# Encoder block on one core: softmax sums carried through the meta keys' transposes, division on GpSimd in each attention unit

## The chip, the core and the metric

The kernel runs on one core of one Trainium2 chip. The metric is the device time of one execution in microseconds (us). TensorE (PE in the profile; PEld is its weight load) multiplies matrices into PSUM, VectorE (DVE) and ScalarE (ACT) read PSUM and SBUF, GpSimd (POOL) here works on SBUF alone, and the SyncE queue (SP) issues most DMAs. Each engine executes its own instructions in order and waits for others through semaphores.

## What is computed

One encoder layer over two batches, a prompt of 256 and a sample of 1024 tokens, each with 16 learned meta tokens in front (lengths 272 and 1040), width 1024, all fp32. Cut to what matters:

```python
h = rms_norm(x, g);  z = h @ w_in            # q | k | v | fourier | two gates
q, k = rope(head_rms_norm(q)), rope(head_rms_norm(k))   # 8 query heads, 2 key/value heads, 64 wide
s = einsum('bqhgd,bshd->bhgqs', qb, k) * scale
p = softmax(s, axis=-1)                      # over all 272 or 1040 keys
a = einsum('bhgqs,bshd->bqhgd', p, v).reshape(..., 512) @ w_attn_o
fo = fourier_mix(f) @ w_four_o
x = x + (sigmoid(g_attn) * a + sigmoid(g_four) * fo) @ w_out
x = x + swiglu_ffn(rms_norm(x));  y = rms_norm(x)       # meta tokens dropped from the output
```

The softmax's division by the sum of the exponentials commutes with the product with v, so it may be applied to the attention output a instead.

## The kernel before

Precision: each fp32 operand of a large product is split into a rounded high part and a low remainder, and three matmuls (L231 to L233) make one product. Work is emitted by Python generators. In the attention the order on PE, ACT and DVE is the order written in the code; DMAs on SP and work on POOL are placed by the framework's scheduler.

**Stages.** First come the norms, transposes, Fourier part and the passes for q and k/v (to about 324 us in the profile); then the attention (324 to about 681), then the merge of the two branches (`merge`, `load_af`), `w_out`, and the feed-forward network to the end.

**Attention** (`attention`, L861 to L1010). A unit is one tile t of 128 queries with one key/value head g: four query heads h. The tiles come in the order 8, 9 (prompt), 0 to 7 (sample), so there are 20 units, 4 of the prompt. For each head: six matmuls (two for the prompt) write the scores into `S` (L960; for the sample one buffer of three PSUM banks, L955); DVE takes the row maximum (L965); ACT takes the exponential into the SBUF slot `p` and, by `accum_out`, the row sum into one column of the small tile `total` (L973). The next head's scores must wait until that exponential has read `S`.

The other half of a unit, `Second`, runs while the next unit's scores run. A `turn` (L889) transposes one block of 128 keys (the ninth block, or third for the prompt, holds the 16 meta keys) of the four heads into a PSUM tile `pt`; ACT rounds it to `pT` (L895), DVE subtracts for the low part (L896). `product` (L906) comes two turns later and adds the block to `pv`, a single PSUM bank of 128 x 512: its upper 64 rows are the product with the high part of v, its lower the other. After the last block ACT copies one half to the slot `ao` (L920), DVE adds the other half (L921), and a DMA stores the sum in DRAM, in `a_d` (L924). In each head `turns(0)` comes behind the maximum and `turns(1)` behind the exponential. Between them the generator yields, and a filler emits matmuls of the gates (`g`, L231 to L233), whose weights are split on ACT and POOL (L578, L579).

**The divisors before.** While the next unit runs, `divide` is called: in its head 1 DVE takes the reciprocals of `total` (L991); in head 2 PE transposes them into a free corner of `S` (L994), DVE copies that (L996), and two DMAs store it in `rc_d` (L999). For the last unit both calls stand ahead of the drain (L1001, L1002). The exponential of head 2 is emitted behind that call.

**Reading a^T back.** `load_af` (L1058) loads 1024 columns of `a_d` (L1070) and the divisors, which a DMA spreads over 64 partitions twice (L1073); DVE multiplies (L1080), and `split` makes the high and low parts (L215, L216). It runs five times: two for chunk 0 (tiles 0 to 3), one for chunk 2 (the prompt), two for chunk 1 (tiles 4 to 7). The merge uses them in the order 0, 2, 1: matmuls `m` behind matmuls `fo` of the Fourier branch.

**Slots.** SBUF is handed out by `Slots` (27 slots of 1056 columns and 7 triples), the one freed longest ago first; whoever writes a slot waits for its last user.

The queries are loaded by `load_q` (L868) from `q_d`, one tile ahead; the first load is emitted when the attention begins.

Of the kernel before, what the change touches and what calls it, by code (L numbers as in the profile page):

```python
# [9 lines left out]
F32 = mybir.dt.float32  # L10
F32R = mybir.dt.float32r
AF = mybir.ActivationFunctionType
ALU = mybir.AluOpType
# [4 lines left out]
P = 128  # L18
# [4 lines left out]
HD = 64  # L23
# [11 lines left out]
CH_N = (512, 512, 256)  # L35
# [22 lines left out]
SLOT = 1056  # L58
# [78 lines left out]
def f32(ap):  # L137
    return ap.bitcast(F32)
# [44 lines left out]
class Kernel:  # L183
    def __init__(self, tc, nc, a, o, pools):
        self.tc, self.nc, self.a, self.o = tc, nc, a, o
        self.const, self.small, self.dram, big = pools
        self.later = None
        self.sl = Slots(big, N_SLOTS, N_TRIPLES)
        c = self.const
        self.ident = c.tile([P, P], F32, name="ident")  # L190
        nc.scalar.dma_start(self.ident[:], a["ident"])
        self.gcol = c.tile([P, KD], F32, name="gcol")
        self.mhalf = c.tile([P, NQH], F32, name="mhalf")
        nc.vector.memset(self.mhalf[:], -0.5)
        self.gates = [
            [self.dram.tile([P, n], F32, name=f"gate{u}_{i}") for i, n in enumerate(CH_N)]
            for u in range(16)
        ]
        self.x_d = [self.dram.tile([P, D], F32, name=f"x_d{t}") for t in range(10)]
        self.act_d = [[self.dram.tile([P, 640], F32, name=f"act_d{j}_{k}") for k in range(NH)] for j in range(7)]  # L200
        self.q_d = [self.dram.tile([P, D], F32, name=f"q_d{t}") for t in range(10)]
        self.a_d = [self.dram.tile([512, n], F32, name=f"a_d{i}") for i, n in enumerate(CH_N)]

        self.rc_d = [self.dram.tile([2, 4 * n], F32, name=f"rc_d{i}") for i, n in enumerate(CH_N)]


        self.f_d = self.dram.tile([516, NL], F32, name="f_d")
# [553 lines left out]
    def kv_pass(self, ps):  # L761
# [14 lines left out]
        for c, off, rows, t in self.TILES[10:] + self.TILES[8:10] + self.TILES[:8]:  # L776
# [33 lines left out]
            if late:  # L810
                late()
                yield 500
            late = post
        yield 8000
        late()
        sl.put(self.rope)
# [41 lines left out]

    def attention(self, ps, tiles, tag_s, tag_v):  # L861


        nc, sl = self.nc, self.sl
        units = [(t, g) for t in tiles for g in range(NKV)]
        q = {}

        def load_q(i):  # L868
            if i < len(tiles) and tiles[i] not in q:
                s = sl.get("qT", F32R)  # L870
                nc.sync.dma_start(f32(s[:, :1024]), self.q_d[tiles[i]][:])
                q[tiles[i]] = s

        load_q(0)

        class Second:

# [11 lines left out]
            def turn(me):  # L889
                V, rows, col = me.keys[me.j]  # L890
                pt = ps.tile([P, 512], F32, tag="tr", name=f"pt{me.t}{me.g}{me.j}")
                for h in range(4):
                    nc.tensor.transpose(pt[:rows, h * P : (h + 1) * P], me.ps4[h][:, col : col + rows], self.ident[:])  # L893
                pT = sl.get("pT", F32R)
                nc.scalar.copy(pT[:rows, :512], pt[:rows, :])  # L895
                nc.vector.tensor_tensor(pT[:rows, 512:1024], pt[:rows, :], f32(pT[:rows, :512]), op=ALU.subtract)  # L896
                if len(late) == 2:
                    product()
                late.append((me, me.j, pT))
                me.j += 1  # L900
                if me.j == len(me.keys):
                    sl.put(*me.slots)
# [3 lines left out]
        def product():  # L906
# [10 lines left out]
                return  # L917
            aos = sl.get("ao")

            nc.scalar.copy(aos[:HD, :512], me.pv[HD:P, :])  # L920
            nc.vector.tensor_tensor(aos[:HD, :512], me.pv[:HD, :], aos[:HD, :512], op=ALU.add)  # L921
            off = (t % 4) * P if t < 8 else (t - 8) * P
            dst = self.a_d[t // 4][:].rearrange("(h d) n -> d h n", d=HD)
            nc.sync.dma_start(  # L924
# [16 lines left out]

        for i, (t, g) in enumerate(units):
            if g == 0:
                load_q(tiles.index(t) + 1)
            if t < 8:
                seq, L, cuts = "s", LS, (0, 264, 776, LS)
            else:
                seq, L, cuts = "p", LP, (0, LP)
            per = SLOT // L
            ps4, slots = [], []  # L950
            total = self.small.tile([P, 4], F32, tag="total", name=f"total{t}{g}", bufs=3)
            for h in range(4):
                hq = q[t][:, (4 * g + h) * P : (4 * g + h + 1) * P]

# [9 lines left out]
                nb = sm[:, 0:1]  # L964
                nc.vector.tensor_reduce(nb, S[:, base : base + L], axis=AX.X, op=ALU.max, negate=True)  # L965
                turns(0)
                if divide and h:
                    divide(S[:4, 0:P] if t < 8 else S[:4, base + 384 : base + 512])
                    divide = None if h == 2 else divide
                if h % per == 0:  # L970
                    slots.append(sl.get("p"))
                p = slots[-1][:, (h % per) * L : (h % per + 1) * L]
                self.last_exp = nc.scalar.activation(p, S[:, base : base + L], AF.Exp, bias=nb, accum_out=total[:, h : h + 1])  # L973
                yield "end" if i + 1 == len(units) else seq, 0, False

                ps4.append(p)
                turns(1)
# [6 lines left out]
                if t == tiles[-1]:  # L984
                    sl.put(*self.kv_slots[:4])
            queue.append((Second(t, g, ps4, slots), n + 1))

            def divide(bank, t=t, g=g, total=total, first=[]):

                if not first:  # L990
                    first.append(nc.vector.reciprocal(total[:], total[:]))  # L991
                    return
                c, off = t // 4, t % 4 * P
                nc.tensor.transpose(bank, total[:], self.ident[:])  # L994
                rc = self.small.tile([4, P], F32, tag="rcT", name=f"rcT{t}{g}")
                nc.vector.tensor_copy(rc[:], bank)  # L996
                for x in range(2):
                    dst = self.rc_d[c][x].rearrange("(k n) -> k n", k=4)[2 * g : 2 * g + 2, off : off + P]
                    nc.sync.dma_start(dst, rc[x::2, :])  # L999

        divide(None)  # L1001
        divide(ps.tile([P, 512], F32, tag="tr", name="rcT")[:4, :P])  # L1002
        while queue:
            for half in range(2):
                turns(half)
# [52 lines left out]
    def load_af(self, c):  # L1058

        nc, sl = self.nc, self.sl  # L1060
        n = CH_N[c]
        per = 1024 // n
        out = self.af[c] = []
        raws = {}

        def load(i):
            if i < 4 // per:
                r, d = raws[i] = sl.get("af"), sl.get("rc")
                src = self.a_d[c][i * per * P : (i + 1) * per * P, :].rearrange("(k p) n -> p k n", p=P)
                nc.sync.dma_start(r.v(per, n), src)  # L1070
                for x in range(2):
                    src = self.rc_d[c][x, i * 1024 : (i + 1) * 1024]
                    nc.sync.dma_start(d[x * HD : (x + 1) * HD, :1024], src.partition_broadcast(HD))  # L1073

        load(0)
        yield 1
        for i in range(4 // per):
            load(i + 1)
            r, d = raws.pop(i)
            nc.vector.tensor_tensor(r[:, :1024], r[:, :1024], d[:, :1024], op=ALU.mult)  # L1080
            out.append(self.split(r, 1024, "af", nc.vector, "t"))
            sl.put(r, d)
            yield 1

    def merge(self, then):
# [854 lines left out]
```

## Time and profile before

| | us |
|---|---|
| median of 3 runs (1744.39 to 1746.44) | 1744.83 |
| the profiled execution's own time | 1742.25 |
| its span, first to last instruction | 1740.5 |
| PE busy | 1667.6 |
| DVE busy | 1093.8 |
| ACT busy | 724.4 |
| POOL busy | 302.8 |

A time in the timeline is counted from the span's start. A row of the timeline is start, duration, engine, line, operation, output and inputs, and in brackets the idle time of the engine just before it with what ended it. A row of the waits is engine, tile and line, what it waited for, the total, the number of times, and the longest. A row of the windows gives the busy time of each engine in a stretch, the clock granted to TensorE (1.00 is full), the busy share of the 16 DMA engines and their GB/s. A matmul's row shows its whole passage; back to back, one with 512 columns starts 0.23 us after the one before it.

### The profile page before, as it was taken

Reading aid. Unit: us, or ns where it says so; the run is one execution under the profiler, and the core shown is the slowest. Engines: PE = TensorE matmul, PEld = TensorE weight load, DVE = VectorE, ACT = ScalarE, POOL = GpSimd, SP = SyncE. Lnnn points to the kernel's source line nnn. Section 1 sums busy time; section 2 is a strip of 40 time slices with the busy share of each in tenths; the row PEclk is TensorE's granted clock in tenths of the full one; section 3 lists DMA queues with packets and bytes.
Section 4 is the critical chain, followed back from the end, with each engine's and each line's share of the span. In section 5 each row is a group of like instructions: output and inputs, shape, how many; then the busy total and the mean of one; then the engine's idle time right before and its main releaser. Section 6 shows DMA issues by size and latency. Waiting matters only on the chain.

```text
span 1740.5 us, 25983 instructions
## 1 busy us (share of the span) xinstructions
PE 1667.6 (96%) x9809; PEld 1479.5 (85%) x9809; DVE 1093.8 (63%) x1973; ACT 724.4 (42%) x1462; POOL 302.8 (17%) x348
## 2 busy tenths in 40 slices
PE   7999999989999999899999999999999999999998
PEld 7888879767777777787879999999999998888886
DVE  5563455346666666663379766676666668775685
ACT  6423233346565665442254322232222234443444
POOL 3350443210021111564244000000000000000002
PEclk9999999999999999899999999999999999999999
DMA  6145221321111218634441223222222237653534
GB/s 244 43 121 176 97 110 58 110 67 51 44 45 41 75 40 244 179 110 169 145 173 61 85 85 102 90 90 93 96 90 87 75 126 253 199 177 105 157 98 154
DMA packets 91581, 198.62 MB, mean 114 GB/s; under 512 B 10006, under 2 KB 41474, under 8 KB 91456
## 3 DMA queue, kind: packets, MB, share of 16 engines
q1 hardware_dynamic: 81552, 179.54, 31.3%
q10 hardware_dynamic: 8400, 12.53, 2.1%
q0 software_dynamic: 1504, 4.89, 0.9%
q8 instruction: 77, 1.26, 0.3%
q14 instruction: 48, 0.39, 0.1%
HBM read 141.46 MB, written 55.46 MB: 113 GB/s over the span
## 4 chain that ended last, share of the span: by engine, by line
PE 60%; DVE 9%; ACT 4%; issue 4%; POOL 2%; DMA 2%; SPq 0%; POOLq 0%; ACTq 0%; DVEq 0%
PE i L231 9%; PE i L233 9%; PE i L232 9%; PE o L233 5%; PE o L232 5%; PE o L231 5%; PE S L960 4%; DVE sm L965 2%; PE pt L893 2%; ACT p L973 2%; PE pv L913 1%; PE wo L232 1%; PE wo L233 1%; PE wo L231 1%; PE g L231 1%
## 5 line engine op out<-in xcount | busy, mean ns | idle before, releaser
L1432 ACT CAST w<-wi 128x512 fp32r<-128x512 f32 x168 | 104.0, 621 | 271.5 <-PE i L233 217.3
L231 PE MATMUL i<-A,w 128*128 128x384 f32 x616 | 208.4, 338 | 3.0 <-ACT w L1432 2.6
L233 PE MATMUL i<-A,w 128*128 128x384 f32 x616 | 208.1, 338 | 2.4 <-POOL w L1434 2.4
L232 PE MATMUL i<-A,w 128*128 128x384 f32 x616 | 207.9, 338 | 0.0
L233 PE MATMUL i<-Ah,w 128*128 128x256 f32 x616 | 173.5, 282 | 0.0
L231 PE MATMUL i<-Ah,w 128*128 128x256 f32 x616 | 173.5, 282 | 0.0
L232 PE MATMUL i<-Al,w 128*128 128x256 f32 x616 | 172.8, 281 | 0.0
L896 DVE TENSOR_TENSOR pT<-pt,pT 128x512 fp32r<-128x512 f32 (+1 forms) x138 | 94.5, 686 | 78.5 <-ACT pT L895 77.3
L240 POOL TENSOR_SCALAR fin0r<-fin0ss 128x1 f32<-128x1 f32 x1 | 0.8, 786 | 755.6 <-ACT X L248 755.6
L1434 DVE TENSOR_TENSOR w<-wi,w 128x512 fp32r<-128x512 f32 x154 | 105.2, 684 | 28.3 <-ACT w L1432 28.0
L965 DVE TENSOR_REDUCE sm<-S 128x1 f32<-128x1040 f32 (+1 forms) x80 | 86.5, 1081 | 55.1 <-PE S L960 51.3
L231 PEld LDWEIGHTS i<-A,w 128*128 128x128 f32 x616 | 116.5, 189 | 3.5 <-ACT w L1432 2.9
L233 PEld LDWEIGHTS i<-A,w 128*128 128x128 f32 x616 | 116.3, 189 | 3.3 <-POOL w L1434 3.2
L231 PEld LDWEIGHTS i<-Ah,w 128*128 128x128 f32 x616 | 116.1, 188 | 0.5 <-ACT w L1432 0.5
L232 PEld LDWEIGHTS i<-A,w 128*128 128x128 f32 x616 | 116.4, 189 | 0.0
L232 PEld LDWEIGHTS i<-Al,w 128*128 128x128 f32 x616 | 116.3, 189 | 0.0
L233 PEld LDWEIGHTS i<-Ah,w 128*128 128x128 f32 x616 | 116.0, 188 | 0.0
L895 ACT CAST pT<-pt 128x512 fp32r<-128x512 f32 (+1 forms) x138 | 80.1, 581 | 82.6 <-PE pt L893 79.2
L973 ACT ACTIVATE p<-S,sm 128x1040 f32<-128x1040 f32 (+1 forms) x80 | 80.1, 1002 | 50.1 <-DVE sm L965 30.2
L893 PE MATMUL pt<-ident,p 128*128 128x128 f32 (+1 forms) x624 | 93.6, 272 | 0.1
L233 PE MATMUL o<-wfo,act 128*128 128x512 f32 (+1 forms) x212 | 82.1, 388 | 2.1 <-DVE act L1566 2.1
L232 PE MATMUL o<-wfo,act 128*128 128x512 f32 (+1 forms) x212 | 82.0, 387 | 0.0
(765 smaller groups left out, 4467.8 us busy)
## 6 DMA issues: line engine op xcount, KB each, us to landing
wi<-w_fi SPq DMA_DIRECT2D x48, 512.0 KB
act_d<-sc SPq DMA_DIRECT2D x77, 192.0 KB
wg<-w_g SPq DMA_DIRECT2D x24, 512.0 KB
act<-act_d SPq DMA_DIRECT2D x37, 320.0 KB
wfo<-w_fo SPq DMA_DIRECT2D x21, 512.0 KB
X<-act_d SPq DMA_DIRECT2D x31, 320.0 KB
act_d<-sc SPq DMA_DIRECT2D x77, 128.0 KB
gt<-gate SPq DMA_DIRECT2D x32, 256.0 KB
```

The lines of the kernel that those rows point to most:

```text
L231: mm(out, sh, mh, start=first and i == 0, stop=False)
L232: mm(out, sh, ml, start=False, stop=False)
L233: mm(out, slo, mh, start=False, stop=last and i == n - 1)
L893: nc.tensor.transpose(pt[:rows, h * P : (h + 1) * P], me.ps4[h][:, col : col + rows], self.ident[:])
L895: nc.scalar.copy(pT[:rows, :512], pt[:rows, :])
L896: nc.vector.tensor_tensor(pT[:rows, 512:1024], pt[:rows, :], f32(pT[:rows, :512]), op=ALU.subtract)
L913: nc.tensor.matmul(me.pv[:], vst, pT[:rows, :512], start=j == 0, stop=False)
L960: nc.tensor.matmul(S[:, base + lo : base + hi], hq, self.kT[seq][g][v][:, lo:hi], start=v == 0, stop=v == 1)
L965: nc.vector.tensor_reduce(nb, S[:, base : base + L], axis=AX.X, op=ALU.max, negate=True)
L973: self.last_exp = nc.scalar.activation(p, S[:, base : base + L], AF.Exp, bias=nb, accum_out=total[:, h : h + 1])
L1432: nc.scalar.copy(w[:, :512], src)
L1434: eng.tensor_tensor(w[:, 512:1024], src, f32(w[:, :512]), op=ALU.subtract)
```

## The change

The exponential's row sum goes into a 17th column behind the meta keys: `p` is one column wider, `accum_out` is that column. At each next head DVE takes the reciprocal of that one column in place. The last turn of a unit transposes 17 columns rather than 16, so that the reciprocals come out as row 16 of `pt`; DVE copies all 17 rows to a new slot `rc`, and one DMA stores row 16 in `rc_d`, which now has one tile for each t. In `product`, a DMA spreads that row over 64 partitions of the same slot; ACT copies one half of `pv` and DVE the other; GpSimd adds them and multiplies by the divisors; then the store to `a_d` as before. The transpose, copy and two stores of `divide`, and in `load_af` the loads of `rc` and the multiplication, are gone; `load_af` emits its first two loads at once. The first load of queries is emitted in `kv_pass`, ahead of that pass's last transposes, and loads run two tiles ahead for the first three tiles.

```diff
-        self.rc_d = [self.dram.tile([2, 4 * n], F32, name=f"rc_d{i}") for i, n in enumerate(CH_N)]
+        self.rc_d = [self.dram.tile([2, 512], F32, name=f"rc_d{t}") for t in range(10)]
...
             late = post
+        self.q = {}
+        self.load_q(8)
         yield 8000
         late()
...
+    def load_q(self, t):
+        if t not in self.q:
+            s = self.q[t] = self.sl.get("qT", F32R)
+            self.nc.sync.dma_start(f32(s[:, :1024]), self.q_d[t][:])
...
-        load_q(0)
+        load_q(1)
...
+                last = me.left() == 1
                 for h in range(4):
-                    nc.tensor.transpose(pt[:rows, h * P : (h + 1) * P], me.ps4[h][:, col : col + rows], self.ident[:])
+                    m = rows + last
+                    nc.tensor.transpose(pt[:m, h * P : (h + 1) * P], me.ps4[h][:, col : col + m], self.ident[:])
                 pT = sl.get("pT", F32R)
+                if last:
+
+                    me.rc = sl.get("rc")
+                    nc.vector.tensor_copy(me.rc[:m, 512:1024], pt[:m, :])
+                    nc.sync.dma_start(self.rc_d[me.t][me.g : me.g + 1, :], me.rc[rows:m, 512:1024])
                 nc.scalar.copy(pT[:rows, :512], pt[:rows, :])
...
             aos = sl.get("ao")
 
+            nc.sync.dma_start(me.rc[:HD, :512], self.rc_d[t][g].partition_broadcast(HD))
             nc.scalar.copy(aos[:HD, :512], me.pv[HD:P, :])
-            nc.vector.tensor_tensor(aos[:HD, :512], me.pv[:HD, :], aos[:HD, :512], op=ALU.add)
+            nc.vector.tensor_copy(aos[:HD, 512:1024], me.pv[:HD, :])
+            nc.gpsimd.tensor_tensor(aos[:HD, :512], aos[:HD, :512], aos[:HD, 512:1024], op=ALU.add)
+            nc.gpsimd.tensor_tensor(aos[:HD, :512], aos[:HD, :512], me.rc[:HD, :512], op=ALU.mult)
+            sl.put(me.rc)
...
             if g == 0:
-                load_q(tiles.index(t) + 1)
+                i0 = tiles.index(t)
+                load_q(i0 + (2 if i0 < 3 else 1))
...
-            per = SLOT // L
+
+            per, wide = SLOT // (L + 1), L + 1
             ps4, slots = [], []
-            total = self.small.tile([P, 4], F32, tag="total", name=f"total{t}{g}", bufs=3)
...
                 turns(0)
-                if divide and h:
-                    divide(S[:4, 0:P] if t < 8 else S[:4, base + 384 : base + 512])
-                    divide = None if h == 2 else divide
+                if divide:
+                    divide()
                 if h % per == 0:
                     slots.append(sl.get("p"))
-                p = slots[-1][:, (h % per) * L : (h % per + 1) * L]
-                self.last_exp = nc.scalar.activation(p, S[:, base : base + L], AF.Exp, bias=nb, accum_out=total[:, h : h + 1])
+                p = slots[-1][:, (h % per) * wide : (h % per + 1) * wide]
+                self.last_exp = nc.scalar.activation(
+                    p[:, :L], S[:, base : base + L], AF.Exp, bias=nb, accum_out=p[:, L:wide]
+                )
                 yield "end" if i + 1 == len(units) else seq, 0, False
+
+                def divide(x=p[:, L:wide]):
+                    nc.vector.reciprocal(x, x)
...
-        divide(None)
-        divide(ps.tile([P, 512], F32, tag="tr", name="rcT")[:4, :P])
+        divide()
...
-                r, d = raws[i] = sl.get("af"), sl.get("rc")
+                raws[i] = sl.get("af")
                 src = self.a_d[c][i * per * P : (i + 1) * per * P, :].rearrange("(k p) n -> p k n", p=P)
-                nc.sync.dma_start(r.v(per, n), src)
-                for x in range(2):
-                    src = self.rc_d[c][x, i * 1024 : (i + 1) * 1024]
-                    nc.sync.dma_start(d[x * HD : (x + 1) * HD, :1024], src.partition_broadcast(HD))
+                nc.sync.dma_start(raws[i].v(per, n), src)
 
         load(0)
+        load(1)
         yield 1
         for i in range(4 // per):
-            load(i + 1)
-            r, d = raws.pop(i)
-            nc.vector.tensor_tensor(r[:, :1024], r[:, :1024], d[:, :1024], op=ALU.mult)
-            out.append(self.split(r, 1024, "af", nc.vector, "t"))
-            sl.put(r, d)
+            raw = raws.pop(i)
+            out.append(self.split(raw, 1024, "af", nc.vector, "t"))
+            sl.put(raw)
             yield 1
```

More of the change, by code (lines that the diff above doesn't have):

```diff
@@ L865, in attention @@
         units = [(t, g) for t in tiles for g in range(NKV)]
-        q = {}
+        q = self.q
         def load_q(i):
[L869 to L872, printed above, removed]
-        load_q(0)
+            if i < len(tiles):
+                self.load_q(tiles[i])
+        load_q(1)
         class Second:
@@ L986, in attention @@
             queue.append((Second(t, g, ps4, slots), n + 1))
[L988 to L996, printed above, removed]
-                for x in range(2):
-                    dst = self.rc_d[c][x].rearrange("(k n) -> k n", k=4)[2 * g : 2 * g + 2, off : off + P]
-                    nc.sync.dma_start(dst, rc[x::2, :])
-        divide(None)
-        divide(ps.tile([P, 512], F32, tag="tr", name="rcT")[:4, :P])
+        divide()
         while queue:
@@ L1067, in load @@
             if i < 4 // per:
-                r, d = raws[i] = sl.get("af"), sl.get("rc")
+                raws[i] = sl.get("af")
                 src = self.a_d[c][i * per * P : (i + 1) * per * P, :].rearrange("(k p) n -> p k n", p=P)
-                nc.sync.dma_start(r.v(per, n), src)
-                for x in range(2):
-                    src = self.rc_d[c][x, i * 1024 : (i + 1) * 1024]
-                    nc.sync.dma_start(d[x * HD : (x + 1) * HD, :1024], src.partition_broadcast(HD))
+                nc.sync.dma_start(raws[i].v(per, n), src)
         load(0)
+        load(1)
         yield 1
         for i in range(4 // per):
-            load(i + 1)
-            r, d = raws.pop(i)
-            nc.vector.tensor_tensor(r[:, :1024], r[:, :1024], d[:, :1024], op=ALU.mult)
-            out.append(self.split(r, 1024, "af", nc.vector, "t"))
-            sl.put(r, d)
+            raw = raws.pop(i)
+            out.append(self.split(raw, 1024, "af", nc.vector, "t"))
+            sl.put(raw)
             yield 1
```

## Prediction, made blind

> **What bounds the kernel now.** I read the page first, then the windows from the attention to the merge, then the waits there, then the timeline of one unit and of the first merge matmuls. Page, part 1:
>
> ```profile
> PE 1667.6 (96%) x9809; PEld 1479.5 (85%) x9809; DVE 1093.8 (63%) x1973; ACT 724.4 (42%) x1462; POOL 302.8 (17%) x348
> ```
>
> PE is the bound, and the whole span holds only 1740.5 - 1667.6 = 73 us of its idle time. A change that takes next to no work from PE can win only idle time, or time at a reduced clock. Where both lie, by windows (stretch, length, busy time with number of instructions, granted clock, DMA share, GB/s):
>
> ```profile
> core 0: us, PE busy (x) PEld busy (x) DVE busy (x) ACT busy (x) POOL busy (x), PEclk, DMA share, GB/s
> 368.00:656.00 288.00, 266.74 (x1563) 211.98 (x1561) 181.56 (x247) 176.00 (x316) 38.37 (x34) 1.00 0.17 50
> ...
> 684.00:690.00 6.00, 6.00 (x32) 6.00 (x31) 5.30 (x6) 3.27 (x6) 2.57 (x2) 0.72 1.04 254
> ...
> 698.00:702.00 4.00, 0.56 (x4) 0.35 (x2) 2.82 (x7) 1.04 (x1) 4.00 (x7) 0.97 1.02 276
> 702.00:710.00 8.00, 6.27 (x13) 3.79 (x13) 5.33 (x7) 3.54 (x6) 1.29 (x1) 0.50 0.81 254
> ```
>
> The sample's attention (368 to 656) has 21.3 us of idle PE, at a quiet DMA (0.17). The start of the merge has DMA at its limit (1.02), PE idle from 698 to 702 and then at half clock. The change works in both places. The waits from 324 to 720, those that bear on it:
>
> ```profile
> ACT p L973 <- DVE rcT L996: 19.6, 19, 1.1
> PEld S L994 <- DVE sm L965: 14.4, 17, 0.9
> DVE ao L921 <- ACT ao L920: 1.7, 1, 1.7
> ACT pT L895 <- POOL wgl L579: 2.9, 2, 1.5
> PE S L960 <- DMA qT<-q_d: 2.2, 1, 2.2
> PE rcT L994 <- DVE total L991: 1.1, 1, 1.1
> ```
>
> **Step 1: `divide` leaves head 2.** The timeline of one such head, and the start of the scores two heads on:
>
> ```profile
> 430.66 1.11 PE L960 MATMUL S<-kT,qT 128*128 128x264 f32 x6
> 431.81 1.24 DVE L965 TENSOR_REDUCE sm<-S 128x1 f32<-128x1040 f32 x1 [0.74 <-PE S L960]
> 432.97 0.68 DVE L896 TENSOR_TENSOR pT<-pt,pT 128x512 fp32r<-128x512 f32 x1
> 433.11 0.27 PE L994 MATMUL S<-ident,total 128*4 128x128 f32 x1 [0.42 <-DVE sm L965]
> 433.57 0.27 DVE L996 COPY rcT<-S 4x128 f32<-4x128 f32 x1
> 433.87 1.13 ACT L973 ACTIVATE p<-S,sm 128x1040 f32<-128x1040 f32 x1 [1.04 <-DVE rcT L996]
> 435.14 1.21 PE L960 MATMUL S<-kT,qT 128*128 128x264 f32 x6 [0.17 <-ACT p L973]
> ...
> 438.94 0.39 PE L960 MATMUL S<-hT0l,qT 128*128 128x264 f32 x1
> ```
>
> PE stands until the maximum is there (0.42), ACT until the corner of `S` is copied (1.04), and the next scores wait for ACT. From scores to scores this takes 435.14 - 430.66 = 4.48; the next head, with the same two turns and no `divide`, takes 438.94 - 435.14 = 3.80. The head loses 0.68. Nineteen of the twenty `divide`s stand in heads: 16 in sample units, 16 x 0.68 = 10.9 us. Three stand in prompt units, where the filler covers part: half of the 1 us that ACT waits (19.6 / 19), 3 x 0.45, 1.3. The last stands ahead of the drain: its PE wait of 1.1 and its own 0.27, 1.4. Together **13.6 us**. Late next is the ordinary chain, scores, maximum, exponential, which is the 3.80 already counted. Bounds: half of it, if PE finds the next wait at once; 21 us, if the other waits of the stage went too, for which I see no reason.
>
> **Step 2: what the attention gets.** Prices:
>
> ```profile
> L991 DVE RECIPROCAL total<-total x20: 157/160/171, 338.3 to 657.8; 128x4 f32<-128x4 f32 x20
> ...
> L846 DVE COPY qT<-qtr x10: 677/691/692, 186.3 to 260.0; 128x512 f32<-128x512 f32 x10
> ...
> L921 DVE TENSOR_TENSOR ao<-pv,ao x20: 681/683/684, 350.2 to 680.9; 64x512 f32<-64x512 f32 x20
> ...
> L579 POOL TENSOR_TENSOR wgl<-wg,wgh x24: 1273/1286/1294, 315.4 to 648.7; 128x512 fp32r<-128x512 f32 x24
> ```
>
> PE: the 17th column is one more column of a weight load; the moving operand, the identity, keeps its 128 columns: 0. DVE per unit: three more reciprocals (3 x 0.16), one copy of 17 x 512 (by L846, 0.69) in the last turn, the copy of a half of `pv` for the sum (0.69 for 0.68), less the copy L996 (0.27): +0.9 us, in stretches where DVE stands. The place of the 17-row copy is ahead of the DVE row here (before it the meta keys' transposes, behind it the last matmul of `pv`):
>
> ```profile
> 423.94 0.60 PE L893 MATMUL pt<-ident,p 128*16 128x128 f32 x4
> ...
> 425.24 0.68 DVE L896 TENSOR_TENSOR hT0l<-pt,hT0l 16x512 fp32r<-16x512 f32 x1 [1.21 <-ACT hT0l L895]
> ...
> 427.62 0.38 PE L914 MATMUL pv<-hT0l,v 16*128 16x512 f32 x1
> ```
>
> DVE has 1.21 us there while ACT rounds, and the copy takes 0.69: 0. Without that cover it is 20 x 0.69 = 13.8. The reciprocals stand behind a turn's subtraction, and the next one waits for ACT as here: 0; uncovered, 60 x 0.16 = 9.6. **Two engines at once** bring `pv` free no sooner: only one of twenty sums waited for ACT's copy (the 1.7 above, in the drain); elsewhere DVE came from the subtraction and starts where it did. Gain 0.6, in the drain.
>
> POOL gets 2 x 1.29 us per unit. It is 13% busy in the stage (38.37 of 288); behind it stand only weight splits, made about a gate unit ahead: 0. SP gets per unit a store of `rc`, a load that waits for that store, and the store of `ao` behind POOL, and loses two. Behind its waits stand weights and queries a unit or more ahead: 0 in the attention.
>
> **What is late** is the slot of `ao`. It is held until its store lands; before, that is the sum (0.68) and a trip through DMA, after it 2 x 1.29 more. The smallest trip in a chain of this trace:
>
> ```profile
> 1440.13 2.05 DMA act_d<-sc
> ```
>
> With it: 0.69 + 1.29 + 1.29 + 2.05 = 5.3 us, if the divisors have landed by then. Following the gets and puts of the old code, a unit takes about 15 slots, one per 1.2 us (a sample unit lasts 288 / 16 = 18 us), and the `ao` slot comes round after 7 gets in most units, 8.4 us: covered. In two units it comes round after 3 or 4, 3.6 to 4.8 us: a stall of 0.5 to 1.7. That ACT does stand for a slot that POOL still reads is in the waits (1.5 us at most, two times). New slots (`rc`, a third query tile) tighten this: I take **-2.5 us**; bounds 0 and -8.
>
> **Step 3: start.** The first scores wait 2.2 us for the queries. Emitted in `kv_pass`, their load has the gates' matmuls of L814 behind it (8000 ns at the share 0.62 of L1743, 5 us): **2.2 us**; bounds 0 (a later weight load takes its place) and 2.2.
>
> **Step 4: merge.** PE's own order, the matmuls `m` of the three chunks:
>
> ```profile
> 692.68 0.39 PE L231 MATMUL m<-afh,pT 128*128 128x512 f32 x1
> 692.91 0.40 PE L232 MATMUL m<-afl,pT 128*128 128x512 f32 x1
> ...
> 696.72 0.38 PE L232 MATMUL m<-afl,pT 128*128 128x256 f32 x1 [0.88 <-DVE afl L216]
> ...
> 701.74 0.77 PE L231 MATMUL m<-wm,pT 128*128 128x512 f32 x1 [3.44 <-ACT wm L215]
> 703.09 0.79 PE L232 MATMUL m<-hT0l,pT 128*128 128x512 f32 x1 [0.58 <-DVE hT0l L216]
> ...
> 706.27 0.80 PE L231 MATMUL m<-wm,pT 128*128 128x512 f32 x1 [0.68 <-ACT wm L215]
> 707.53 0.80 PE L232 MATMUL m<-afl,pT 128*128 128x512 f32 x1 [0.46 <-DVE afl L216]
> 708.12 0.63 PE L233 MATMUL m<-wm,pT 128*128 128x512 f32 x1
> 708.55 0.63 PE L231 MATMUL m<-wm,pT 128*128 128x512 f32 x1
> ...
> 709.83 0.48 PE L1145 MATMUL fo<-hT0l 68*128 68x328 f32 x1
> ```
>
> From 692.68 to 709.83 are 17.15 us. At the spacing of the first two rows (0.23, half for 256 columns) the 36 matmuls need 12 x 0.23 + 12 x 0.12 + 12 x 0.23 = 7.0. The other 10.2 are waits for the splits of a^T (6.0) and half clock. Why the splits are late:
>
> ```profile
> L1080 DVE TENSOR_TENSOR af<-af,rc x5: 1217/1259/1755, 684.1 to 703.9; 128x1024 f32<-128x1024 f32 x5
> ```
> ```profile
> 696.41 7.44 DMA rc<-rc_d
> ```
>
> Five multiplications of 1.26 stand before the splits on DVE, and the last waits for a load of `rc` that takes 7.44. Both go; the 2.6 MB of ten such loads (256 KB each), some 10 us at the 254 to 276 GB/s above, move to where DMA is at 0.17. Against it: the last unit's `a_d` row comes later, by POOL's 2 x 1.29 less DVE's 0.6, and by divisors that now go out and back through a busy queue; and the load of that half of a^T, emitted earlier, can hold the loads behind it on SP. So the last of the splits still waits. Gain at least 0, at most 10.2; I take **7**.
>
> A rule bears on the clock here. The rows: half clock (0.50) follows a gap of 3.44 us, but the window from 684 (0.72) holds a fall too, with PE busy all through it. The Trainium skill, "TensorE: Matmul & The Clock Gate", Part 1, says that about 3.4 us of idling halve the clock and about 3.4 us of work restore it. The first row agrees, the second does not. By that rule a remaining wait that is one gap of over 3.4 us would be paid for again at half clock.
>
> **Sum.** 13.6 + 0.6 - 2.5 + 2.2 + 7 = 20.9 us. The profiled execution took 1742.25 us, so 1721.4 after; it stands 2.6 below the median 1744.83, so the median comes to **1724 us**.
>
> **Rivals.**
> - *The merge keeps its wait.* The last unit's divisors cross DMA at share 1.02, twice, at up to the 7.44 shown for one load; then the last half of a^T lands when it did. For: those rows. Against: 2.6 MB fewer in that stretch. Step 4 gives 0: 1731.
> - *The gap stays in one piece and the clock falls again.* As forecast, but what is left of step 4's wait is one gap behind which PE runs at half clock: the 12 `m` of 512 columns lose 12 x (0.43 - 0.23) = 2.4 us again (0.43 is the spacing of the rows at 708), and some 8 `fo` behind them 8 x 0.20 x 328/512 = 1.0: 1727.4. For: the half clock behind 3.44.
> - *All of step 4, no stall for slots.* 10.2 and 0: 1718. For: DVE and DMA both lose their load there.
> - *The cover is missing.* The reciprocals and the 17-row copy land on the chain from maximum to exponential, so that the wait only changes its name: 13.8 us back, 1738. For: ACT now stands 1 us each time for just such a DVE copy. Against: the new copy stands ahead of a subtraction with 1.21 us of idle time, and the exponential doesn't read its result.
> - *Slower: slots in every unit.* Divisors go to DRAM and back before POOL can multiply, and then `ao` goes out: three trips of x us in a row from the last turn. In the rows of step 2 `pt` is there at 424.5 and `pv` ends at 428.0, two turns later; so the slot is held 3x - 0.9 us from the end of `pv`, against the 8.4 it has. It decides from x = 3.1 us; at x = 3.6 every unit's rounding or exponential stands 1.5 us, 20 x 1.5 = 30: 1754. For: big loads take 4 us and more in this trace. Against: these are 2 to 128 KB at share 0.17, and the near row is 2.05.
>
> **Chances.** Forecast 0.46; merge keeps its wait 0.17; clock falls again 0.12; all of step 4 0.10; cover missing 0.09; slower 0.06. A measurement of this kernel can tell about 0.2%, 3.5 us, from no change. The missing cover counts 0.03 as faster (1738) and 0.06 as the same, where step 4 fails with it (1745). So faster 0.88; same 0.06; slower 0.06. The range runs from 1714 (all of step 4 and 4 us of the stage's other idle time) to 1738 (the missing cover alone); it leaves out 0.12 above and a little below.
>
> **What would show it.** Right: no ACT wait at L996's place, head 2 as long as heads 0 and 3; the sample's attention about 11 us shorter; the first scores without a wait for queries; no gap of 3 us among the first `m`, and no window at 0.50. Wrong: ACT or DVE waiting in `pT` or `p` for a DMA or for POOL in many units (slots); the 17-row copy with ACT's rounding done before it; `m` of the last chunk waiting for an `a_d` that is late.

## The result, and the profile after

The changed kernel takes 1726.03 us (median of 4 runs, 1724.94 to 1727.52); the kernel before, run beside it, 1745.05 (4 runs, 1744.39 to 1746.44). The ratio is 0.9891, with a 95% interval of 0.9873 to 0.9908: 19 us less, where 20.9 were forecast. The profiled execution took 1726.55 us, its span 1724.7; against the profile of before (1742.25) that is 15.7 less, because the profile of before lies 2.8 below its median and this one 0.5 above. The stages of the two profiles, by starts on PE; the last column is what was gained.

| Stage | before | after | gained |
|---|---|---|---|
| start to the first product for k and v | 253.2 | 252.2 | 1.0 |
| to the first scores | 71.0 | 67.7 | 3.3 |
| scores of the prompt | 44.3 | 43.6 | 0.7 |
| sample: first scores of its first head to those of its last | 284.5 | 277.5 | 7.0 |
| to the first `m` | 39.8 | 40.7 | -0.9 |
| first `m` to the `fo` behind the third chunk | 17.15 | 7.26 | 9.9 |
| to the end of the span | 1030.7 | 1035.7 | -5.1 |

The last row is code that the change does not touch. From that `fo` to the last `o` it took between 1023.4 and 1029.6 us in the fourteen profiles of this study (1023.8 before, 1028.8 after, 1023.4 in a kernel that holds most of the change). So most of it is put down to the spread of executions, and the experiments below, where they can, go by the medians of several runs. The kernel before and the two experiments that start from it lie low, though (1023.8 to 1025.6), and the rows above the last add up to 20.9 where the medians gained 19: a cost of one or two us behind the merge is not excluded.

The page's first part, after:

```profile
PE 1660.4 (96%) x9789; PEld 1479.8 (86%) x9789; DVE 1101.2 (64%) x2028; ACT 725.6 (42%) x1462; POOL 353.2 (20%) x388
```

PE has twenty matmuls less (the transposes of `total`) and is still the bound. DVE has 55 instructions more, for 7 us; POOL has 50 us more. Now the windows of the sample's attention, of four microseconds in its first unit, and of the merge's start (stretch, length, busy times, granted clock, DMA share, GB/s):

```profile
core 0: us, PE busy (x) PEld busy (x) DVE busy (x) ACT busy (x) POOL busy (x), PEclk, DMA share, GB/s
364.00:641.00 277.00, 260.02 (x1522) 211.07 (x1520) 187.58 (x290) 175.44 (x313) 78.16 (x65) 0.99 0.18 55
...
368.00:372.00 4.00, 4.00 (x17) 3.09 (x16) 1.91 (x3) 1.86 (x4) 0.99 (x1) 0.58 0.00 0
...
681.00:687.00 6.00, 6.00 (x34) 5.10 (x33) 5.33 (x8) 3.68 (x6) 5.56 (x7) 1.00 0.70 234
687.00:693.00 6.00, 5.86 (x33) 4.82 (x32) 3.75 (x7) 1.58 (x3) 2.66 (x3) 1.00 0.58 183
```

Idle PE time in the sample's attention went from 21.3 to 17.0 us. At the merge's start PE hardly stands, and the half clock of before is gone; but there is a new stretch at 0.58 in the first unit of the sample. The waits from 320 to 690, those that answer to the ones shown of before and those that are new:

```profile
PEld S L977 <- ACT p L989: 22.3, 37, 2.3
PEld pv L925 <- DVE ao L934: 10.7, 16, 1.0
ACT pT L907 <- DVE rc L905: 8.7, 11, 3.1
PE pv L925 <- DVE ao L934: 6.5, 12, 0.8
...
ACT pT L907 <- POOL ao L936: 3.1, 1, 3.1
...
PE fo L231 <- ACT hT0l L1124: 2.4, 1, 2.4
...
ACT p L989 <- DVE p L995: 2.0, 2, 1.3
```

ACT's 19.6 us behind `rcT` and PE's waits for `sm` and `total` at L994 are gone. The reciprocals that took their place stop ACT twice, for 2.0 us together. New are ACT's waits for the 17-row copy (L905), eleven in the row shown and fifteen, 12.4 us, with the other slots that `pT` is handed, and one long one for GpSimd's product (L936). The timeline of one head 2, and the start of the scores behind it:

```profile
429.96 1.23 PE L977 MATMUL S<-kT,hT0l 128*128 128x264 f32 x6
431.23 1.24 DVE L982 TENSOR_REDUCE sm<-S 128x1 f32<-128x1040 f32 x1
432.50 1.13 ACT L989 ACTIVATE p<-S,sm 128x1040 f32<-128x1040 f32 x1 [0.21 <-DVE sm L982]
432.98 0.15 DVE L995 RECIPROCAL p<-p 128x1 f32<-128x1 f32 x1
433.77 0.39 PE L977 MATMUL S<-hT0l,qT 128*128 128x264 f32 x1
```

Scores, maximum, exponential, scores, with nothing between: 3.81 us, where it was 4.48. The merge, in PE's timeline (the first `m` of each chunk, and the `fo` behind the third):

```profile
681.70 0.39 PE L231 MATMUL m<-afh,y 128*128 128x512 f32 x1
...
684.48 0.29 PE L231 MATMUL m<-afh,y 128*128 128x256 f32 x1
...
685.93 0.39 PE L231 MATMUL m<-wm,y 128*128 128x512 f32 x1
686.29 0.50 PE L232 MATMUL m<-hT0l,y 128*128 128x512 f32 x1
...
688.96 0.32 PE L1147 MATMUL fo<-hT0l,y 68*128 68x328 f32 x1
```

The 36 matmuls follow one another in 7.26 us, 0.3 from the 7.0 that their spacing allows.

### The profile page after: what moved, and what is told of

It is laid out like the page before. It is cut to its first block, busy times and chain, and to the rows that moved or that the text cites. A ratio compares the mean times of both kernels' runs of the same rounds, so it can differ in the third digit from the quotient of the medians.

```text
span 1724.7 us, 26106 instructions
## 1 busy us (share of the span) xinstructions
PE 1660.4 (96%) x9789; PEld 1479.8 (86%) x9789; DVE 1101.2 (64%) x2028; ACT 725.6 (42%) x1462; POOL 353.2 (20%) x388
## 4 chain that ended last, share of the span: by engine, by line
PE 48%; DVE 6%; issue 3%; POOL 2%; ACT 2%; DMA 1%; SPq 0%; POOLq 0%; DVEq 0%; ACTq 0%
PE i L231 9%; PE i L233 9%; PE i L232 9%; PE o L233 5%; PE o L232 5%; PE o L231 5%; PE wo L232 1%; PE wo L233 1%; PE wo L231 1%; POOL gt L1228 1%; POOL wol L216 1%; DVE wi L1415 1%; DVE A L1375 0%; DVE h L1378 0%; DVE fst L1167 0%
## 5 line engine op out<-in xcount | busy, mean ns | idle before, releaser
L908 DVE TENSOR_TENSOR pT<-pt,pT 128x512 fp32r<-128x512 f32 (+1 forms) x118 | 80.7, 685 | 62.1 <-ACT pT L907 61.7
L907 ACT CAST pT<-pt 128x512 fp32r<-128x512 f32 (+1 forms) x118 | 68.7, 582 | 78.8 <-PE pt L900 60.4
L233 PE MATMUL o<-wfo,act 128*128 128x512 f32 (+1 forms) x212 | 82.3, 389 | 2.0 <-DVE act L1568 2.0
L900 PEld LDWEIGHTS pt<-ident,p 128*128 128x128 f32 (+1 forms) x624 | 72.7, 135 | 13.2 <-DVE pT L908 2.8
```

What stands on the lines that cost most here:

```text
L233: mm(out, slo, mh, start=False, stop=last and i == n - 1)
L900: nc.tensor.transpose(pt[:m, h * P : (h + 1) * P], me.ps4[h][:, col : col + m], self.ident[:])
```

## The experiments

The theory after this reading: steps 1 and 4 of the forecast hold, step 1 to the size. What the sample's attention fell short of 11 us is one slot stall and one stretch at half clock, not the new copies on DVE. The rivals: the new copies cost time; the start's gain is more than the queries; the merge's gain is the earlier load or the traffic. Differences below are between medians; ratios are to the kernel before, run beside each.

**The 17th column alone** (`col17`), in the kernel before:

```diff
+ last = me.left() == 1          # transposes take m = rows + last columns
+ if last:
+     rc = self.small.tile([32, 512], F32, tag="rcT", ..., bufs=1)
+     nc.vector.tensor_copy(rc[:m, :], pt[:m, :])
+     # row 16 to the old rc_d: one DMA per parity of the head
- accum_out=total[:, h : h + 1]
+ accum_out=p[:, L:wide]         # and nc.vector.reciprocal(x, x) behind each head
```

> The kernel before with the 17th column alone: sums beside the probabilities, reciprocals per head, the 17-row copy, and the row of divisors stored by two DMAs into the old layout. ACT's copy of the upper half and DVE's sum, the division in the merge, the loads of the queries are as before (slots of 1044 words instead of 1056, so that the copy has a tile of its own). Theory (my step 1 is right, and the 4 us that the attention lost again come from slots of ao): heads 2 of the sample 0.69 us shorter each, sample's attention 284.5 - 11.0 = 273.5 us, merge as before at 17.15 us from the first m to fo; 1745.0 - 13.6 = 1731.5 us, 1729 to 1734. Rival A (the copy of 17 rows, ahead of ACT's rounding of the same bank, costs time): attention about 277.5 as in the changed kernel, 1735.5 us. Rival B (the cover is missing altogether): 1745 us.

1730.87 us (1730.11 to 1734.1); ratio 0.9928 (0.9915 to 0.9940), 13.8 us less. The mean step from scores to scores, by head of the sample's 16 units, from the starts on PE:

```
             head 0   head 1   head 2   head 3   whole stage
before        3.93     5.60     4.57     3.92      284.48
col17         3.94     5.62     3.88     3.91      273.55
after         3.92     5.71     3.88     4.09      277.54
```

Head 2 becomes 0.69 shorter on the mean of the sixteen, and the other heads stay, though ACT waits here, too, for the copy of 17 rows (waits of this kernel from 364 to 641):

```profile
ACT pT L906 <- DVE rc L900: 4.8, 9, 2.8
```

The merge takes 16.86 us, as before. So step 1 is worth 11 us in the sample, and both rivals fall. The other 2.8 of the 13.8 are not to be found where the forecast had them: the prompt's scores take 45.0 us (44.3 before; the clock at their start is 0.85 here and 1.00 there, about 0.6 us of it), from the last head to the first `m` it is 39.2 (39.8), and the profiles differ by 11.8 in all. What the changed kernel lacks against this run (4 us) sits in heads 1 and 3: 6.20 instead of 4.63 in head 1 of the first unit, and one step of 6.91 in a head 3.

**One slot.** That step, in the timeline of the changed kernel:

```profile
511.92 1.28 POOL L935 TENSOR_TENSOR ao<-ao 64x512 f32<-64x512 f32 x1 [1.96 <-DVE p L995]
513.27 0.72 POOL L1045 CAST hT0l<-x64r 4x656 fp32r<-4x656 f32 x1
...
516.50 2.13 POOL L1045 CAST y<-x64r 4x1024 fp32r<-4x1024 f32 x2
518.70 1.28 POOL L936 TENSOR_TENSOR ao<-ao,rc 64x512 f32<-64x512 f32 x1
...
520.01 0.58 ACT L907 CAST pT<-pt 128x512 fp32r<-128x512 f32 x1 [3.14 <-POOL ao L936]
```

GpSimd adds at 511.92, then works through 5.4 us of the Fourier branch's tails, which the scheduler has put between sum and product, and multiplies at 518.70. ACT stands 3.14 us for the slot. Three kernels ask what of it counts. In the first, DVE adds as before (`dve_add`):

```diff
- nc.vector.tensor_copy(aos[:HD, 512:1024], me.pv[:HD, :])
- nc.gpsimd.tensor_tensor(aos[:HD, :512], aos[:HD, :512], aos[:HD, 512:1024], op=ALU.add)
+ nc.vector.tensor_tensor(aos[:HD, :512], me.pv[:HD, :], aos[:HD, :512], op=ALU.add)
```

> The changed kernel with DVE's sum of the two halves as before (DVE adds pv's lower half to ACT's copy); GpSimd only multiplies. Theory (two engines do not copy halves of one bank at once; DVE waits for ACT in both forms): no loss in pv's release, one GpSimd instruction of 1.28 us less in each unit, so the slot of ao comes back 1.28 sooner and the drain's end up to 1.3 us sooner: 1726.0 - 1.3 = 1724.7 us, 1722 to 1726.5. Rival A (the change's claim: the copies run beside each other): each unit 0.6 us longer, 20 x 0.6 = 12, 1738 us. Rival B (my forecast's own 0.6 us in the drain): 1726.6 us.

1723.59 us (1721.74 to 1724.18); ratio 0.9880 (0.9867 to 0.9894). The second (`ao_own`) does that and keeps `ao` outside the pool:

```diff
- aos = sl.get("ao")
+ aos = self.small.tile([P, 512], F32, tag="ao", name=f"ao{t}{g}", bufs=1)
- sl.put(aos)
```

> As the run before it (DVE adds, GpSimd multiplies), and ao in a tile of its own outside the pool of slots (slots of 1044 words instead of 1056 make room). Theory (the step of 6.9 us at 517 us is a slot that GpSimd's late multiplication still holds): no wait of ACT for GpSimd's ao in the attention, 3.1 us less than the changed kernel there: with the 1.3 us of the drain 1726.0 - 3.1 - 1.3 = 1721.6 us, 1719 to 1723. Rival (the pool was short by one slot anyway; ACT stands for the next holder instead): as the run before it, 1724.7 us.

1719.02 us (1717.44 to 1721.69); ratio 0.9857 (0.9844 to 0.9871). The third (`own_only`) keeps every instruction of the change and moves only `ao`'s tile; DVE's half goes to the half of the divisors' slot that held the 17-row copy:

> The changed kernel with all its instructions, both copies of pv's halves and GpSimd's sum and product; only ao's tile lies outside the pool of slots (slots of 1044 words; DVE's half goes into the unused half of the divisors' slot, which stays in the pool). Theory (the 6.9 us step hangs on ao's slot, which GpSimd holds until its product): the step is gone, 3.1 us less: 1726.0 - 3.1 = 1722.9 us, 1720 to 1724. Rival A (it hangs on GpSimd's queue, behind whose late product the divisors' slot is held just as long): the stall stays, 1726 us. Rival B (all of the 7 us by which the run with DVE's sum and ao's own tile is faster come from the pool): 1719 us.

1723.59 us (1721.19 to 1726.21); ratio 0.9882 (0.9863 to 0.9901). The 6.91 us step takes 4.00, 3.86 and 3.86 us in the three, and the sample's attention 273.0, 273.4 and 273.4. In `own_only` the product is as late as before, and ACT doesn't wait (its timeline):

```profile
518.22 0.59 ACT L907 CAST y<-pt 128x512 fp32r<-128x512 f32 x1 [0.80 <-PE pt L900]
...
518.25 1.30 POOL L936 TENSOR_TENSOR ao<-ao,rc 64x512 f32<-64x512 f32 x1
```

So it was the slot of `ao`, 3.1 us once; the divisors' slot, held just as long, and GpSimd's late product cost nothing. That DVE's sum alone is enough shows how thin it is: there the product ends at 516.26 instead of 519.98, and the slot's next user waits only 0.23 for it. `ao_own` came out 2.6 us under its expectation and 4.6 under the two others, with the same attention. Against `own_only` the drain explains most: from the last head's scores to the first `m` that takes 42.3 us, `ao_own` 39.2, because in `own_only` DVE's half stands 2.02 us until the store of the divisors' row has left its place. Against `dve_add` the profiles differ by 1.4 us among the first `m` (PE waits 1.11 there once) and by 3.4 behind them, and that is left open.

**Two engines on one bank.** `dve_add` answers for the two copies as well. PE's wait for `pv` to come free, from 364 to 655, first in the changed kernel, then in `dve_add`:

```profile
PEld pv L925 <- DVE ao L934: 9.5, 14, 1.0
...
PE pv L925 <- DVE ao L934: 5.9, 10, 0.8
```
```profile
PEld pv L925 <- DVE ao L934: 9.5, 14, 1.0
...
PE pv L925 <- DVE ao L934: 5.9, 10, 0.8
```

The same to a tenth of a microsecond. The copies do not run beside each other: in the drain of the changed kernel, where both engines are free, DVE begins when ACT has ended (timeline):

```profile
668.48 0.58 ACT L933 COPY ao<-pv 64x512 f32<-64x512 f32 x1 [0.97 <-PE pv L926]
669.09 0.68 DVE L934 COPY ao<-pv 64x512 f32<-64x512 f32 x1 [1.20 <-ACT ao L933]
```

Neither reads what the other writes; they share the bank of `pv`, and the slot `ao` that they write. The same holds for `pt`, where ACT's rounding waits for the 17-row copy, and there the two write different tiles (`pT` and `rc`), so it does not take a common target. The Trainium skill, "PSUM — Partial Sum Buffer", section "PSUM bank collisions raise a hardware error", says that two engines on one bank and the same 32 partitions collide, reads against reads included, and that the compiler's scheduler sets such accesses one after the other. It names different partitions as free of this; the halves of `pv` lie in different ones, and here they wait all the same, which would fit an order kept by whole banks (or by whole tiles; `pv` fills its bank, so these runs cannot tell).

**Which reads `pt` first** (`round_first`): on `ao_own`, with `nc.scalar.copy(pT[:rows, :512], pt[:rows, :])` emitted ahead of the block `if last:`.

> The fastest so far (DVE's sum, GpSimd's product, ao in a tile of its own) with ACT's rounding of the last block emitted ahead of the 17-row copy, so that the copy waits for ACT in the same bank and not the other way. Theory (the serial reading of one bank, 0.67 us, is covered by other work either way): 1719.0 us, 1717.5 to 1720.5. Rival (ACT's 11 waits for the copy, 8.7 us in all in the changed kernel, reach PE): 4 to 8 us less, 1713 us.

1718.64 us (1716.6 to 1719.2); ratio 0.9851 (0.9834 to 0.9869): as `ao_own`. Now DVE waits for ACT, so the serial reading is real in either order, and in sum the order is worth nothing. One head shows a cost all the same. In the sample's first unit the copy stands behind the row maximum on DVE, ACT's rounding behind the copy, the exponential behind both, and the next scores wait for that (timeline of the changed kernel):

```profile
376.39 0.58 ACT L907 CAST pT<-pt 16x512 fp32r<-16x512 f32 x1 [3.12 <-DVE rc L905]
...
378.13 0.39 PE L977 MATMUL S<-hT0l,qT 128*128 128x264 f32 x1 [0.98 <-ACT p L989]
```

That head 2 takes 4.75 us in the changed kernel and 4.74 in `ao_own`, but 3.69 in `round_first`. The other heads of the sample, most of them heads 1, together take 0.7 longer there, so little of the 1.05 is left.

**The queries** (`q_old`), in the changed kernel:

```diff
- self.load_q(8)                            # in kv_pass, ahead of its last 8000 ns of filler
- load_q(1)
+ load_q(0)                                 # when the attention begins
- load_q(i0 + (2 if i0 < 3 else 1))
+ load_q(tiles.index(t) + 1)
```

> The changed kernel with the loads of the queries as before: the first at the attention's start, then one tile ahead. Theory (step 3 as forecast, 2.2 us): the first scores stand 2.2 us for the queries, 1726.0 + 2.2 = 1728.2 us. Rival A (the early load is worth the 4.2 us by which the first sample scores came sooner): 1730.2 us. Rival B (the slot that a third query tile holds costs as much in the attention, by the 6.9 us step at 517 us that goes with it): 1725 us, the start 2.2 later and the attention 3 shorter.

1730.45 us (1729.61 to 1731.42); ratio 0.9921 (0.9908 to 0.9935): 4.4 us more, the size of rival A. From the first product for k and v to the first scores it takes 71.1 us instead of 67.7. That is no spread: it is 70.9 to 71.1 in the four profiles with the late load (before, `col17`, `nodiv`, `q_old`) and 67.6 to 67.7 in the ten with the early one. Of these 3.4 us, 2.4 are the wait for the queries and 0.4 a wait of the last transposes `ktr` for DVE, which the early load does not have; why is not taken apart. The wait for the queries has about the size of before; what follows it has not. First the timeline's wait and the windows in `q_old`, then the windows of before:

```profile
323.27 0.49 PE L975 MATMUL S<-kTp,qT 128*128 128x272 f32 x2 [2.38 <-DMA qT<-q_d]
```
```profile
320.00:324.00 4.00, 1.62 (x9) 1.13 (x8) 0.78 (x3) 1.02 (x3) 0.00 (x0) 1.00 0.93 330
324.00:328.00 4.00, 4.00 (x12) 3.09 (x12) 0.24 (x1) 0.58 (x2) 0.00 (x0) 0.58 0.47 181
```
```profile
320.00:324.00 4.00, 1.51 (x7) 0.91 (x7) 1.18 (x5) 1.46 (x6) 0.00 (x0) 1.00 0.76 259
324.00:328.00 4.00, 3.87 (x19) 3.28 (x20) 0.68 (x2) 0.58 (x2) 0.00 (x0) 1.00 0.99 390
```

PE stands for 2.2 to 2.4 us in both; then the clock is 0.58 for four microseconds in the one (4 x 0.42 = 1.7 us) and 1.00 in the other. The prompt's scores take 45.2 us in `q_old` and 43.6 in the changed kernel. So the start of `q_old` is 3.4 + 1.6 = 5.0 us longer in the profiles; against the kernel before, without the fall, the early load gained 3.3 + 0.7 = 4.0. `q_old` also has a longer slot stall (4.6 us), so rival B's price for a third query tile isn't there.

**The merge.** The division left out of it, in the kernel before (`nodiv`): no loads of `rc`, no `tensor_tensor(r, r, d, op=ALU.mult)`; a^T goes on undivided.

> The kernel before with the division left out: the merge neither loads divisors nor multiplies, so a^T goes on undivided; everything else, the early load of the second half excepted, is as before. Theory (the merge's gain is the division's leaving): from the first m to the fo behind the third chunk about 7.3 us instead of 17.15, as in the changed kernel; 1744.7 - 9.9 = 1734.8 us, 1734 to 1737. Rival (the load of the second half, emitted earlier, brings it): the 3.4 us gap stays, 1742 to 1745 us.

1734.53 us (1731.03 to 1736.14); ratio 0.9942 (0.9925 to 0.9959): 9.9 us less, and 6.95 us from the first `m` to the `fo`. The rest of the change isn't needed for it. Then its two halves, put back into the changed kernel. The multiplications (`mult`), each of a tile by itself, so that the result is the square:

```diff
  raw = raws.pop(i)
+ nc.vector.tensor_tensor(raw[:, :1024], raw[:, :1024], raw[:, :1024], op=ALU.mult)
```

> The changed kernel with five DVE multiplications of 128 x 1024 put back into the merge, each a tile of a^T by itself, so that the result is the square; no loads of divisors. Theory M (DVE's multiplications in front of the splits were the larger part): 5 x 1.26 = 6.3 us on DVE, of which PE sees 4 to 6.3: 1726.0 + 5 = 1731 us. Theory D (the loads of 256 KB were): 0 to 1 us, 1726.5 us.

1735.93 us (1733.17 to 1741.67), 9.9 more than the changed kernel; ratio 0.9953 (0.9938 to 0.9969). Of that 7.4 stand in the stretch, which takes 14.66 us instead of 7.26, with the gap and the half clock of before (0.61 from 690 to 698). That is more than theory M's 4 to 6.3: the five take 1.22 to 1.76 us each, and the clock comes on top (timeline of PE):

```profile
687.07 0.39 PE L232 MATMUL m<-afl,y 128*128 128x256 f32 x1 [0.99 <-DVE afl L216]
...
691.43 0.80 PE L231 MATMUL m<-wm,y 128*128 128x512 f32 x1 [2.79 <-ACT wm L215]
692.69 0.80 PE L232 MATMUL m<-hT0l,y 128*128 128x512 f32 x1 [0.46 <-DVE hT0l L216]
```

The loads, first with slots of their own kind (`loads`), then without (`dram_loads`, the destination a scratch tile in DRAM):

```diff
+ d = sl.get("rc")                          # dram_loads: self.dram.tile([HD, 1024], F32, ...)
+ src = self.rc_d[8].rearrange("a b -> (a b)")
+ for x in range(2):
+     nc.sync.dma_start(d[x * HD : (x + 1) * HD, :1024], src.partition_broadcast(HD))
+ sl.put(d)
```

> The changed kernel with ten loads of 256 KB put back into the merge, a row of divisors broadcast to half the partitions, beside the loads of a^T; nothing reads them. Theory D (these 2.6 MB, 10 us at 260 GB/s, made a^T late): 5 to 9 us more, 1733 us. Theory M (the multiplications did): 0 to 2 us, 1727 us.

> The changed kernel with ten transfers of 256 KB beside the loads of a^T, a row of divisors broadcast from DRAM into scratch in DRAM that nothing reads: the traffic of the old loads without their slots. Theory M (the multiplications made nearly all of the merge's gain; the run with the loads in slots lost 12 us by a slot in the drain, not by traffic): 0 to 2 us more, 1727 us. Theory D (the traffic itself makes a^T or the weights late): 5 to 9 us more, 1733 us.

`loads`: 1738.52 us (1736.51 to 1740.07); ratio 0.9967 (0.9955 to 0.9980). That misses both theories, and not in the merge, which takes 6.98 us: the first `m` comes 15 us late, since in the drain the copy of 17 rows waits for a slot that one of these loads is filling (DVE's timeline):

```profile
659.19 0.68 DVE L905 COPY rc<-pt 17x512 f32<-17x512 f32 x1 [13.05 <-DMA rc<-rc_d]
```

`dram_loads`: 1726.31 us (1724.67 to 1728.74); ratio 0.9898 (0.9881 to 0.9914), as the changed kernel; the stretch takes 8.43 us, with one wait of 1.1. But this run does not ask what it was built to ask. Nothing holds these transfers back, and the scheduler issued all ten some 300 us ahead of the merge (SyncE's instructions at their line):

```profile
352.80 2.49 SPq L1079 DMA_DIRECT2D d<-rc_d  x4
362.88 0.49 SPq L1079 DMA_DIRECT2D d<-rc_d  x1
365.22 3.13 SPq L1079 DMA_DIRECT2D d<-rc_d  x5
```

And the wait of 1.1 stands in `dve_add` too (1.11, a stretch of 8.40), which has no such transfers. In `loads` six of the ten are issued from 680 to 690, but there the slot in the drain had already made the merge 15 us late. So the multiplications alone bring back 7.4 of the 9.9; the other 2.5 may be the loads, the two together, or the spread: kernels with neither take 6.95 to 8.43 for this stretch. What the traffic of the loads was worth beside the loads of a^T no run here shows. In the kernel before, the merge waits for `rc` itself once, for 0.8 us.

**The early load of the second half** (`late_load`): `load(1)` back behind the first split.

> The changed kernel with the load of the second half of a^T emitted where it was, behind the first split. Theory (with the division gone it is in time in either place): 1726.0 us, 1725 to 1727.5. Rival (it is a trip through DMA late, and PE stands for it at the last chunk, with the half clock behind): 2 to 4 us more, 1729 us.

1723.65 us (1721.26 to 1725.41); ratio 0.9881 (0.9866 to 0.9897), whose interval overlaps that of the changed kernel: no loss, perhaps a gain.

**All together** (`best`): DVE's sum, `ao` in its own tile, rounding first, late load.

> DVE's sum, GpSimd's product, ao in a tile of its own, ACT's rounding ahead of the 17-row copy, and the load of the second half of a^T behind the first split as before. Theory (the last load's place is worth nothing; the 2.4 us by which that run alone was under the changed kernel are the spread of runs): 1718.8 us, 1717 to 1720.5. Rival (the early load delays the loads behind it and its removal is worth those 2.4 us): 1716.3 us.

1717.11 us (1715.12 to 1727.62); ratio 0.9854 (0.9832 to 0.9876). That is not to be told from `ao_own` or `round_first`, so the late load is worth nothing that these runs can measure. The three are the fastest of the study, 25 to 28 us below the kernel before and 7 to 9 below the change.

## Why the prediction came out right

The time lies 2.0 us above the forecast and inside the range. The mechanisms of steps 1 and 4 are those of the forecast. That the sum comes so close is in part luck: most of its terms are off, in both directions.

- **Step 1, 13.6: right in size and place in the sample, the rest not shown.** 0.68 per head was forecast, 0.69 measured, 10.9 in all. The 1.3 of the prompt's units does not show in `col17`, where a lower clock hides part of it, and of the drain's 1.4 it has 0.6; its median of 13.8 is the forecast's total, but its stages do not add up to it.
- **Step 2, the 17-row copy, 0: nearly right in the sample, for another reason.** The prediction put it into DVE's 1.21 us of idle time beside ACT's rounding. It isn't beside it: ACT waits for it in fifteen of the twenty units. It costs next to nothing, by the timeline because `product` uses the block two turns later, and `round_first` shows that the order is in sum all one; in one head it cost 1.05.
- **The drain, two gains forecast, 0.9 lost.** From the last head's scores to the first `m` the change takes 40.7 us, the kernel before 39.8. The five kernels with GpSimd's sum and the slots of the change take 40.2 to 41.6 (`loads` left out), the four with DVE's sum 39.0 to 40.0. The difference of the means, 1.2, is about GpSimd's one instruction of 1.28 us, so the 0 given to its work does not hold there.
- **Two engines at once, 0.6: failed.** In the drain DVE waited 1.20 us for ACT.
- **Slots, -2.5: near in size, 3.1, by luck; wrong in its reason.** The prediction reckoned with the trip of the divisors through DMA and with two units of few gets. It was one unit, and the time went in GpSimd's queue, between its two instructions; the 0 given to GpSimd's work counted its busy share and not the order in which it stands.
- **Step 3, 2.2: the wait was right, the sum too small.** `q_old` puts 4.4 on it. Missing were about 1 us more ahead of the first scores and, in `q_old`, the clock behind them.
- **Step 4, 7: mis-sized, 9.9.** The step that failed is the sentence that the last of the splits still waits. Nothing waits there in the changed kernel's profile; with the multiplications gone DVE is early, and the last half of a^T is there in time although the store comes behind GpSimd. The prediction named multiplications and loads without weighing them; the multiplications alone bring back 7.4, and the share of the loads is open.
- **Not in the forecast:** 1.57 us in head 1 of the sample's first unit, at a clock of 0.58. `col17`, `dve_add` and seven others have the same wait there, and no fall.

Of the rivals, the one that kept the merge's wait is out by the changed kernel's own rows, the one of the clock by its windows at the merge (1.00), and the one of the missing cover by `col17`, one head excepted. "All of step 4" was nearly right about step 4 and wrong about the slots. The slower one had a real mechanism: `loads` shows what one slot that waits for a transfer costs, 13 us. In the change a slot was waited for once, for 3.1, and behind GpSimd.

## What to carry to other kernels

A small operation between the maximum and the exponential is paid in full by the engine that bounds; the same work placed where its result is used two turns later was nearly free here, even though it makes another engine wait. When work is moved to an engine with time to spare, look at what the scheduler puts between its instructions and at what they hold meanwhile: a buffer of its own outside the shared pool took that cost away here. Ahead of a stage's first matmuls, five DVE instructions of 1.22 to 1.76 us, 7.2 in all, cost PE 7.4. And when a run puts something back to price it, look in its profile where the scheduler placed it: the ten transfers of `dram_loads` ran 300 us before the stage that they were meant to burden.

## What the runs showed of the hardware

The clock falls after gaps of 1.9 to 2.4 us in some executions and not in others. At the start of the sample PE stands 1.9 us in all fourteen profiles, before the same matmuls. In five of them (the change, `q_old`, `mult`, `late_load`, `round_first`) the next four microseconds run at 0.57 or 0.58, in nine at 1.00. Here is that stretch of `loads`, whose code is that of the change up to the drain, and in which DMA is as quiet behind the gap:

```profile
364.00:368.00 4.00, 2.12 (x12) 1.51 (x11) 1.31 (x2) 1.95 (x4) 1.32 (x2) 1.00 0.66 197
368.00:372.00 4.00, 4.00 (x22) 3.08 (x21) 2.22 (x4) 2.60 (x5) 1.25 (x1) 1.00 0.00 0
```

The same stretch ran at 0.58 in one execution and at 1.00 in another, at a price of 1.6 us. Behind the wait of 2.2 to 2.4 us for the queries the clock fell in three of four profiles (`q_old` 0.58, `col17` 0.85, `nodiv` 0.50 from 324 to 328) and not in the kernel before. A kernel with several such gaps can get a spread of its own from this; no kernel here was profiled twice. The Trainium skill, "TensorE: Matmul & The Clock Gate", Part 1, says that the gate watches a free-running window, which the difference between executions fits, and that about 3.4 us of idling halve the clock, which these gaps of 1.9 to 2.4 us do not bear out.
